# RWKV-7 scan of a diffusion trunk on one core: chunk batches of all head pairs in one series, merge inside a pair's first batch, transfers of the inverse on three queues

## The chip, the cores and the metric

One NeuronCore of one Trainium2 chip runs the whole program. The metric is the device time of one execution in microseconds (us); lower is better. Three runs of the kernel before gave 2060.2, 2059.9 and 2052.24 us, with a median of 2059.9 us.

## What is computed

Two trunk layers over 512 latent tokens (a 64-wide grid) and 256 context tokens of width 1024, all in float32. Layer 0 mixes by a bidirectional RWKV-7 recurrence (8 heads of 64) beside windowed attention, layer 1 by neighbourhood attention beside global attention. Each layer ends in a squared-ReLU MLP of width 4096, and each sub-layer is modulated by vectors that a product of the conditioning with `w_ada` gives. The part that matters here is the recurrence of layer 0, run once forwards and once backwards, the context tokens ahead of the latent ones:

```
def step(state, inp):
    r_t, w_t, k_t, v_t, kk_t, a_t = inp
    sa = jnp.einsum('bhvk,bhk->bhv', state, -kk_t)
    state = (state * w_t[:, :, None, :] + sa[..., None] * (kk_t * a_t)[:, :, None, :]
             + v_t[..., None] * k_t[:, :, None, :])
    return state, jnp.einsum('bhvk,bhk->bhv', state, r_t)
```

## The kernel before, in words

**The scan.** The 768 tokens are cut into 12 chunks of 64, and the 8 heads into 4 pairs (`p` = 0 to 3). Inside a chunk the recurrence is solved by matrix products, for which the inverse of a 64x64 triangular matrix is needed per chunk, head and direction. Three pieces of work make up a pair:

- `prep(p)` (L843) is a generator. Up to its mark FRONT it loads `r` and `k` and makes the norm, the decays and the rates. Up to READY it writes the factors `ar` and `bk` (L903, L908, L942, L945) and multiplies them on TensorE (L917), with the masked result in `XI` (L918). SP stores the 32x32 diagonal blocks of `XI` to DRAM in another layout (L925, four transfers) and loads them as `N` on 96 partitions (L928). From READY to MERGE VectorE inverts the blocks in 31 dependent steps of two instructions (L954, L955), copies the result transposed (L958), and SP stores both (L959, L960) and loads them back into `XI` and `xw` (L966, L967). After MERGE, TensorE and ScalarE join the 32x32 inverses to 64x64 ones (L974, an ACT copy, L982, an ACT copy).
- `chunks(p)` (L989) works in 4 batches of 3 chunks. Of a batch, `factors` (L1017), `masked` (L1046), `own` (L1062) and `solved` (L1071) come one batch ahead of `local` (L1082), `passed` (L1104) and the three `step`s (L1120), which hand the state on. `solved` is the first that reads the merged `XI`.
- `mix_out(p)` (L1177) takes the pair's output `y` and stores it. Pair 3 has `bonus` and `mix_last` in its place.

**Buffers.** `ar`, `bk`, `XI`, `wc`, `kds` lie in two sets, one for even and one for odd pairs. All of these products go through two PSUM tiles of two banks each (`wide()`, named `b` in the trace). `py` (two banks) gathers a pair's output, `pd` (one bank) carries the state product, and `ad` (one bank) belongs to the modulation.

**Order.** The kernel's text fixes each instruction's rank. The framework plans each engine's queue from these ranks, and every queue then runs in order, waiting where data or a buffer is late. Before the scan, the loop at L1484 runs `prep(1)` to READY and then the merge of pair 0 (L1486). For each pair, `for _ in cg` (L1532) walks the 37 yields of `chunks(p)`. At each it advances the background `bg` by RATE3 = 1.8 steps and the modulation `ag` by RATE4 = 0.7. The background takes turns between the inverse of pair p+1, `mix_out(p-1)` and `prep(p+2)` to FRONT. When the pair's chunks are through, `rest()` (L1542) runs `prep(p+2)` to READY and then the merge of pair p+1. Only then do the chunks of pair p+1 begin.

**The modulation.** `ada` (L332) streams 96 tiles of 512 KB of `w_ada` through three buffers on SP's queue (L341) and multiplies them (L353, L362); some 76 of them fall into the scan or just ahead of it.

Of the kernel before, what the change touches and what calls it, by code (L numbers as in the profile page):

```python
# [11 lines left out]
F32 = mybir.dt.float32  # L12
# [8 lines left out]
KT = 8  # L21
# [153 lines left out]
def trunk(ctx: ExitStack, tc: tile.TileContext, xT, cT, vec_d, wada, we, wo_in, wout, wf1, wf2, lw2_d, la2_d, lg2_d,  # L175
# [5 lines left out]
    def act(o, i, f=AF.Copy, **k):  # L181
        return S.activation(o, i, f, **k)  # L182
# [660 lines left out]
    def prep(p, R, rt, iv, sts, res):  # L843
# [77 lines left out]
        for d in range(2):  # L921
            for b in range(2):
                o = d * 64 + b * 32
                i0 = d * 48 + b * 24
                nc.sync.dma_start(nscr[p, i0:i0 + 24].rearrange("i s t -> s i t"), xv[o:o + 32, :, 32 * b:32 * b + 32])  # L925

        N = iv.tile([128, 32, 32], F32, name="N")
        nc.sync.dma_start(N[0:96], nscr[p])  # L928
        X = iv.tile([128, 32, 32], F32, name="X")
        G.memset(X[0:96], 0.0)  # L930
        G.memset(X[0:96].rearrange("p a b -> p (a b)")[:, 0::33], 1.0)
# [14 lines left out]
            yield QUIET  # L946
        G.tensor_tensor(kds, kds, kd, op=ALU.add)
        stt(kds, kds, VV["rk"][:, p:p + 1], r, op0=ALU.mult, op1=ALU.mult)
        yield READY
        for s in range(31):  # L950
            a, b = s + 1, 31 - s
# [4 lines left out]
            if s % 2:  # L956
                yield QUIET if s > QS else None
        V.tensor_copy(N[0:96].rearrange("p s i -> p i s"), X[0:96])  # L958
        nc.sync.dma_start(xscr[p], X[0:96])  # L959
        nc.sync.dma_start(tscr[p], N[0:96])  # L960
        w1 = rt.tile([128, T], F32, name="xw")
        for d in range(2):
            for b in range(2):
# [1 line left out]
                i0 = d * 48 + b * 24  # L965
                nc.sync.dma_start(xv[o:o + 32, :, 32 * b:32 * b + 32], xscr[p, i0:i0 + 24].rearrange("i s t -> s i t"))  # L966
            nc.sync.dma_start(w1[d * 64:d * 64 + 32].rearrange("s (i t) -> s i t", t=32), tscr[p, d * 48:d * 48 + 24].rearrange("i s t -> s i t"))  # L967
        res[p] = (AR, BK, XI, wc, kds)
        yield MERGE
        for q in range(2):  # L970
            pw = one()
# [14 lines left out]

    NB = 3

    def chunks(p, y, ct, pch, res):  # L989

# [7 lines left out]
        ch = (FWD, BWD)  # L998
        v = ct.tile([128, T], F32, name="v")
        nc.sync.dma_start(v, scr[3 + 3 * p + 2])  # L1000
        py = pch.tile([128, 2, 512], F32, name="py")
        pd = pch.tile([128, 128], F32, name="pd")
        yp = py[:, :, 0:384].rearrange("p h (c f) -> p h c f", f=64)
        B = [{} for _ in range(NCH // NB)]
        last = None
        env = {}
# [75 lines left out]
        def local(b):  # L1082

            BT, Z = B[b]["BT"], B[b]["Z"]
            pn = wide()[:, 0:NB * 128].rearrange("p (i d v) -> p i d v", i=NB, d=2)
            for i in range(NB):
                for d in range(2):
                    for h in range(2):
                        PE.matmul(pn[half(h), i, d], BT[:, h, d * NB + i, 0:64], Z[:, i, d, h], start=True, stop=True)
            N = B[b]["N"] = ct.tile([128, NB, 2, 64], F32, name="Nb", bufs=2)  # L1090
            act(N, pn)
            for i in range(NB):
# [27 lines left out]
        def step(b, i):  # L1120
            nonlocal X
            s = NB * b + i
            N = B[b]["N"][:, i]
            if not s:
                X = N
                return
            MQ, St = B[b]["MQ"], X
            if s < NCH - 1:
                for d in range(2):
# [11 lines left out]
        for b in range(nb + 1):  # L1141
            if b < nb:
                factors(b)
                yield
            if b:
                local(b - 1)
                yield
            if b < nb:
                masked(b)
                yield  # L1150
            if b:
                passed(b - 1)
                yield
            if b < nb:
                own(b)
                yield
            if b:
                step(b - 1, 0)
                yield
            if b < nb:  # L1160
                solved(b)
                yield
            if b:
                for i in range(1, NB):
                    step(b - 1, i)
                    yield
        act(y.rearrange("p c (h f) -> p h c f", h=2), yp)
        yield

    def centred(y):  # L1170

# [298 lines left out]
    with ExitStack() as p2:  # L1470
# [10 lines left out]
            if t != QUIET:  # L1481
                next(ag, None)
        gate = mix_gate(tl)
        for t in until(preps[1], READY):  # L1484
            next(ag, None)
        for t in preps[0]:  # L1486
            next(ag, None)
        for p in range(4):
            cg, n = chunks(p, y, ct, pch, res), 0

            def turns(*gs):
                gs = list(gs)
                while gs:
                    for g in list(gs):
                        t = next(g, gs)
                        if t is gs:
                            gs.remove(g)
                        else:
                            yield t

            def behind():
                def out():
                    return mix_out(p - 1, y, gate, tl, res) if p else iter(())
                if p < 3:
                    yield from turns(until(preps[p + 1], MERGE), out(), front(p + 2))
                else:
                    yield from out()
                    for x in mixs[::-1]:
                        x.close()
                    p3w["W"] = ffstream(p3w["x"].enter_context(pool("wp3")), 0)  # L1510
                    m0 = p3w["m0"] = p3w["m"].enter_context(pool("m0"))
                    p3w["last"] = m0.tile([128, T], F32, name="last")
                    yield from bonus(3, tl, res, gate, p3w["last"])
                    mh = m0.tile([128, KT, 256], F32R, name="mh")
                    ml = m0.tile([128, KT, 256], F32R, name="ml")
                    p3w["mh"] = mh, ml
                    for j in range(8):
                        for _ in range(3):
                            yield
                        p3w["W"].ahead(j + 1)  # L1520
                        if j in (5, 6):
                            a, b = ((4, 8), (0, 3))[j - 5]
                            if a:
                                mr = m0.tile([128, 4, 256], F32, name="mr")
                            else:
                                mr = tl.tile([128, T], F32, name="t", bufs=2).rearrange("p (k t) -> p k t", k=3)
                            nc.sync.dma_start(mr, mixd[a:b, :, 0:256].rearrange("k p t -> p k t"))
                            split(mh[:, a:b], ml[:, a:b], mr)
            bg = behind()
            due = [0.0, 0.0]  # L1530
            t = None
            for _ in cg:  # L1532
                n += 1
                due[0] += RATE3
                due[1] += RATE4
                while due[0] >= 1:
                    due[0] -= 1
                    next(bg, None)
                while due[1] >= 1:
                    due[1] -= 1  # L1540
                    next(ag, None)
            def rest():  # L1542
                if p < 2:
                    yield from until(preps[p + 2], READY)
                if p < 3:
                    yield from preps[p + 1]
            for t in itertools.chain(bg, rest()):
                due[1] += RATE5
                while due[1] >= 1:
                    due[1] -= 1  # L1550
                    next(ag, None)
        for _ in ag:
            pass
        end = mix_last(3, y, tl, p3w["last"], p3w["gate"], mk)
# [336 lines left out]
```

## Time and profile before

| what | value |
|---|---|
| runs | 2060.2, 2059.9, 2052.24 us; median 2059.9 us |
| profiled execution, its own time | 2055.19 us |
| its span, first to last instruction | 2053.4 us |
| TensorE busy (PE) | 1932.7 us, 94% of the span |
| VectorE busy (DVE) | 1124.7 us, 55% |
| ScalarE busy (ACT) | 817.0 us, 40% |
| GpSimd busy (POOL) | 122.2 us, 6% |
| mean granted clock of TensorE | 0.971 |
| DMA | 217.47 MB, 106 GB/s on the mean |

Everything below is from the profiled execution, with time counted from the start of its span. Busy time is the union of an engine's instructions. Matmuls overlap in the engine, so a busy PE can still wait between instructions. A sequencer's own work (waits, DMA issues) is not counted as busy. The granted clock is 1.00 at 2.4 GHz, and a stretch at 0.75 had half its time at 1.2 GHz.

### The profile page before, as it was taken

How to read it: one execution, taken by the hardware profiler on the slowest of the kernel's cores; microseconds unless marked ns; L12 is line 12 of the kernel's file. 1: busy time of each engine (PE TensorE's matmuls, PEld its weight loads, DVE VectorE, ACT ScalarE, POOL GpSimd, SP SyncE). 2: the span in 40 equal slices, each digit the busy share in tenths (PEclk: the TensorE clock that was granted, in tenths of full speed). 3: DMA queues.
4: the chain of work that ended last, by engine and by line, in shares of the span. 5: the costliest groups of instructions: out<-in, count | busy, mean ns of one | idle time of the engine just before them, and what ended most of it. 6: DMA issues, size and time to landing. Idle time of an engine off the chain costs nothing.

```text
span 2053.4 us, 38620 instructions
## 1 busy us (share of the span) xinstructions
PE 1932.7 (94%) x16412; PEld 1633.5 (80%) x16412; DVE 1124.7 (55%) x1999; ACT 817.0 (40%) x1531; POOL 122.2 (6%) x149
## 2 busy tenths in 40 slices
PE   6999988988888899999999999899999899999997
PEld 3878767666666897888888889898888798888887
DVE  6576477547464377233433345856575575444445
ACT  3466442534335244311322122435686645222332
POOL 1000011011100000000000000001021000000000
PEclk9999989999999999999999999999999999999998
DMA  7422334666634233211221021342111334322221
GB/s 309 149 65 78 108 109 129 209 195 207 207 126 145 71 112 132 73 61 42 83 72 62 32 83 42 103 151 68 51 39 37 123 102 166 102 83 82 97 88 42
DMA packets 112013, 217.47 MB, mean 106 GB/s; under 512 B 38496, under 2 KB 63968, under 8 KB 111328
## 3 DMA queue, kind: packets, MB, share of 16 engines
q1 hardware_dynamic: 96544, 191.66, 28.6%
q10 hardware_dynamic: 15296, 23.33, 3.2%
q8 instruction: 129, 2.11, 0.4%
q14 instruction: 44, 0.36, 0.1%
HBM read 184.29 MB, written 28.05 MB: 103 GB/s over the span
## 4 chain that ended last, share of the span: by engine, by line
PE 63%; DVE 7%; ACT 3%; issue 3%; DMA 2%; POOL 1%; POOLq 0%; ACTq 0%; DVEq 0%; SPq 0%
PE x L1588 45%; PE x L430 5%; PE ax L530 2%; PE ax L511 2%; PE b L1015 1%; PE b L493 1%; PE ad L353 1%; PE b L1077 1%; PE b L494 1%; DMA w_raw<-in_wada_dram 1%; DVE X L955 1%; DVE nacc L288 1%; ACT Z L182 1%; DVE pr L954 1%; POOL r L264 0%
## 5 line engine op out<-in xcount | busy, mean ns | idle before, releaser
L182 ACT ACTIVATE w_hi<-w_raw 128x1024 fp32r<-128x1024 f32 x183 | 192.3, 1058 | 484.1 <-PE x L1588 369.1
L225 DVE TENSOR_TENSOR w_lo<-w_raw,w_hi 128x1024 fp32r<-128x1024 f32 x181 | 220.8, 1223 | 194.6 <-ACT w_hi L182 193.0
L1588 PE MATMUL x<-fl,w_hi 128*128 128x256 f32 (+1 forms) x864 | 290.9, 338 | 3.9 <-DVE fl L1675 3.9
L1588 PE MATMUL x<-uh,w_hi 128*128 128x512 f32 (+1 forms) x864 | 286.7, 337 | 3.0 <-ACT uh L182 3.0
L1588 PE MATMUL x<-fh,w_lo 128*128 128x256 f32 (+1 forms) x864 | 289.4, 336 | 0.0
L1588 PE MATMUL x<-ul,w_hi 128*128 128x512 f32 (+1 forms) x864 | 287.9, 336 | 0.0
L1588 PE MATMUL x<-uh,w_lo 128*128 128x512 f32 (+1 forms) x864 | 287.6, 336 | 0.0
L1588 PE MATMUL x<-fh,w_hi 128*128 128x256 f32 (+1 forms) x864 | 286.9, 337 | 0.0
L1602 DVE TENSOR_TENSOR oa<-x,oa 128x512 f32<-128x512 f32 (+1 forms) x184 | 103.1, 563 | 207.9 <-PE x L1588 207.0
L430 PE MATMUL x<-uh,w_hi 128*128 128x256 f32 (+1 forms) x560 | 190.2, 340 | 1.6 <-ACT po L182 1.3
L430 PE MATMUL x<-uh,w_lo 128*128 128x256 f32 (+1 forms) x560 | 189.1, 338 | 0.0
L430 PE MATMUL x<-ul,w_hi 128*128 128x256 f32 (+1 forms) x560 | 188.5, 337 | 0.0
L1588 PEld LDWEIGHTS x<-fl,w_hi 128*128 128x128 f32 x864 | 164.3, 190 | 22.0 <-DVE fl L1675 4.3
L1588 PEld LDWEIGHTS x<-uh,w_hi 128*128 128x128 f32 x864 | 161.8, 189 | 21.1 <-ACT uh L182 3.9
L1588 PEld LDWEIGHTS x<-fh,w_lo 128*128 128x128 f32 x864 | 164.1, 190 | 17.9
L1588 PEld LDWEIGHTS x<-fh,w_hi 128*128 128x128 f32 x864 | 162.1, 190 | 20.0 <-ACT fh L182 2.5
L1588 PEld LDWEIGHTS x<-ul,w_hi 128*128 128x128 f32 x864 | 162.8, 189 | 17.7
L1588 PEld LDWEIGHTS x<-uh,w_lo 128*128 128x128 f32 x864 | 162.8, 189 | 17.6
L430 PEld LDWEIGHTS x<-uh,w_hi 128*128 128x128 f32 x560 | 107.5, 192 | 12.5 <-issue 2.7
L430 PEld LDWEIGHTS x<-uh,w_lo 128*128 128x128 f32 x560 | 107.7, 192 | 9.4 <-issue 1.2
L430 PEld LDWEIGHTS x<-ul,w_hi 128*128 128x128 f32 x560 | 107.8, 192 | 9.2 <-issue 1.3
L1674 DVE TENSOR_TENSOR rl<-rl 128x512 f32<-128x512 f32 (+1 forms) x108 | 59.3, 550 | 77.7 <-ACT fh L182 77.5
(304 smaller groups left out, 3398.7 us busy)
## 6 DMA issues: line engine op xcount, KB each, us to landing
w_raw<-in_wf_dram SPq DMA_DIRECT2D x128, 512.0 KB
w_raw<-in_wada_dram SPq DMA_DIRECT2D x96, 512.0 KB
w_raw<-in_we_dram SPq DMA_DIRECT2D x21, 512.0 KB
w_raw<-in_wo_in_dram SPq DMA_DIRECT2D x18, 512.0 KB
w_raw<-in_wout_dram SPq DMA_DIRECT2D x16, 512.0 KB
hsc<-h ACTq DMA_DIRECT2D x8, 1024.0 KB
scr<-po ACTq DMA_DIRECT2D x21, 384.0 KB
h<-hsc SPq DMA_DIRECT2D x7, 1024.0 KB
```

The lines of the kernel that those rows point to most:

```text
L182: return S.activation(o, i, f, **k)
L225: eng.tensor_tensor(o_lo, x, o_hi.bitcast(F32), op=ALU.subtract)
L288: V.tensor_reduce(acc, sq.rearrange("p k t -> p t k"), axis=AX.X, op=ALU.add)
L353: PE.matmul(ps[o:o + 32, 0:256], si[:, 2 * kp + k, :], w[:, k, j * 256:(j + 1) * 256], start=kp == 0, stop=kp == 3)
L430: PE.matmul(ps[:, 0:b - a], x, y, start=j == 0, stop=j == len(pairs) - 1)
L493: PE.matmul(ps[:, off:off + n], qs, kh, start=True, stop=False)
L494: PE.matmul(ps[:, off:off + n], qs, kl, start=False, stop=True)
L511: PE.transpose(pt[:, (kb - k0) * 128:(kb - k0 + 1) * 128], P[:, kb * 128:(kb + 1) * 128], ident)
L530: PE.matmul(po[h * 64:h * 64 + 64, 0:128], v(h, k), pts[h][:, k], start=k == 0, stop=k == n - 1)
L1588: PE.matmul(o, a, b, start=n == 0, stop=n == len(pairs) - 1)
L1602: tt(oa[:, m, tok], ps, oa[:, m, tok], op=ALU.add)
L1674: tt(r, r, r, op=ALU.mult)
```

## The change

The chunk stages become functions that `stages(p)` returns, and one generator `batches` walks 16 batches `g` of all pairs. In a round it takes `factors`, `masked`, `own`, `solved` of batch g and `local`, `passed` and the steps of batch g-1, whichever pair they belong to. When the first batch of a pair comes to `solved`, `batches` yields MERGE. Then the background is emptied, `prep(p+1)` to READY and the merge of pair p are emitted in turns, and a new background begins. In that background the inverse has two places in the turn. The loop that took `prep(1)` to READY ahead of the scan is gone; that part heads pair 0's background. `py` is allocated at the pair's first `local`, `pd` at each step. The four stores of `XI` move from SP's queue to ACT's, and the load of `N` and the two stores of the result move to POOL's.

```
-                nc.sync.dma_start(nscr[p, i0:i0 + 24].rearrange("i s t -> s i t"), xv[o:o + 32, :, 32 * b:32 * b + 32])
+                nc.scalar.dma_start(nscr[p, i0:i0 + 24].rearrange("i s t -> s i t"), xv[o:o + 32, :, 32 * b:32 * b + 32])
...
-        nc.sync.dma_start(N[0:96], nscr[p])
+        G.dma_start(N[0:96], nscr[p])
...
+        res[p] = (AR, BK, XI, wc, kds)
         yield READY
...
-        nc.sync.dma_start(xscr[p], X[0:96])
-        nc.sync.dma_start(tscr[p], N[0:96])
+        G.dma_start(xscr[p], X[0:96])
+        G.dma_start(tscr[p], N[0:96])
...
-    def chunks(p, y, ct, pch, res):
+    def stages(p, y, ct, pch, res, done_y):
...
-        py = pch.tile([128, 2, 512], F32, name="py")
-        pd = pch.tile([128, 128], F32, name="pd")
...
+            if s == NCH - 1:
+                act(y.rearrange("p c (h f) -> p h c f", h=2), yp)
+                done_y.append(p)
+        return factors, masked, own, solved, local, passed, step
+
+    def batches(y, ct, pch, res, done_y):
+        nb = NCH // NB
...
+        pairs[0] = stages(0, y, ct, pch, res, done_y)
+        for g in range(4 * nb + 1):
+            new, old = g < 4 * nb, 0 < g
+            work = [new and (FACTORS, g), old and (LOCAL, g - 1), new and (MASKED, g), old and (PASSED, g - 1), new and (OWN, g),
+                      old and (STEP, g - 1, 0), new and (SOLVED, g), old and (STEP, g - 1, 1), old and (STEP, g - 1, 2)]
+            for w in filter(None, work):
+                if w[0] == SOLVED and not g % nb:
+                    yield MERGE
+                f, b = of(w[1], w[0])
+                f(b, *w[2:])
                 yield
+                if w[0] == FACTORS and g % nb == nb - 1 and g < 4 * nb - 1:
+                    p = g // nb + 1
+                    pairs[p] = stages(p, y, ct, pch, res, done_y)
...
-        for t in until(preps[1], READY):
-            next(ag, None)
         for t in preps[0]:
             next(ag, None)
...
+        def behind(p):
+            if p < 3:
+                if p == 0:
+                    yield from until(preps[1], READY)
+                inverse = until(preps[p + 1], MERGE)
+                yield from turns(inverse, outputs(p - 1), inverse, front(p + 2))
+                return
...
+        for t in batches(y, ct, pch, res, done_y):
+            if t == MERGE:
+                for _ in bg:
+                    modulation(RATE5)
+                if p:
+                    for _ in turns(until(preps[p + 1], READY) if p < 3 else iter(()), preps[p]):
+                        modulation(RATE5)
+                bg, p = behind(p), p + 1
+                continue
+            modulation(RATE4)
+            due[0] += RATE3
+            while due[0] >= 1:
+                due[0] -= 1
+                next(bg, None)
```

`outputs(p)` is `mix_out(p)` once `done_y` holds p. RATE5 is 0.5.

## Rows read from the trace of the kernel before

**Rows 1.** The page's picture of the span in 40 equal slices of 51.3 us: busy tenths of TensorE, and the granted clock in tenths.

```profile
PE   6999988988888899999999999899999899999997
...
PEclk9999989999999999999999999999999999999998
```

**Rows 2.** Busy time by stretch, core 0. Columns: stretch and its length, busy us and instructions of PE, PEld, DVE, ACT and POOL, granted clock, DMA share, GB/s. The cuts are at 345.5 (end of the input products), 357.0 (first merge), 375.7, 469.0, 570.2 and 645.0 (factors of the second batch of pairs 0 to 3), and 434.1, 533.1 and 617.1 (end of the last `solved` of pairs 0 to 2). The last row is one batch of pair 3, from `factors` to `solved`, with no other work beside it.

```profile
345.50:357.00 11.50, 6.51 (x129) 4.32 (x127) 11.02 (x15) 2.09 (x6) 4.69 (x3) 0.70 0.63 192
357.00:375.70 18.70, 16.20 (x360) 13.49 (x356) 4.97 (x11) 9.43 (x19) 0.46 (x2) 0.73 0.60 166
375.70:434.10 58.40, 52.12 (x937) 36.53 (x940) 40.30 (x96) 25.14 (x44) 6.21 (x7) 1.00 0.71 226
434.10:469.00 34.90, 32.20 (x692) 21.52 (x685) 14.77 (x29) 11.81 (x26) 4.06 (x4) 0.90 0.66 195
469.00:533.10 64.10, 55.72 (x917) 41.15 (x918) 44.30 (x100) 26.89 (x47) 8.95 (x9) 0.92 0.59 191
533.10:570.20 37.10, 32.27 (x692) 21.29 (x684) 14.56 (x27) 11.93 (x26) 4.01 (x4) 0.91 0.67 207
570.20:617.10 46.90, 41.63 (x839) 31.75 (x840) 33.79 (x89) 15.25 (x33) 3.34 (x5) 1.00 0.42 129
617.10:645.00 27.90, 23.73 (x493) 18.66 (x486) 11.15 (x16) 14.12 (x26) 3.12 (x3) 0.82 0.35 102
...
672.50:683.00 10.50, 10.11 (x260) 9.15 (x260) 3.31 (x6) 4.16 (x9) 0.00 (x0) 1.00 0.01 3
```

**Rows 3.** Timeline of TensorE where the scan begins. Columns: start, length (us), engine, line, operation, shapes, count, and in brackets the idle time before it and what ended it.

```profile
345.90 0.50 PE L362 MATMUL ad<-con,adar 128*128 128x4 f32 x4
348.81 0.69 PE L917 MATMUL b<-ar,bk 64*64 64x64 f32 x8 [2.40 <-DVE po L1429]
...
357.05 1.99 PE L974 MATMUL b<-xw,XI 32*32 32x32 f32 x96
...
364.70 1.54 PE L1023 MATMUL b<-con,bk 128*128 128x128 f32 x6
```

**Rows 4.** Groups of TensorE's instructions by line between 434.1 and 469.0 us. Columns: line, engine, operation, tiles, shapes, count, then busy us and mean ns of one, then idle us before them.

```profile
L353 PE MATMUL ad<-w_raw,si 128*32 128x256 f32 x104 | 9.2, 429 | 1.7 <-DMA w_raw<-in_wada_dram 1.3 <-DVE mod L364 0.3
L917 PE MATMUL b<-ar,bk 64*64 64x64 f32 x96 | 3.3, 227 | 0.3 <-DVE ar L903 0.3
L982 PE MATMUL b<-XI,xw 32*32 32x32 f32 x96 | 2.5, 205 | 0.0
...
L974 PE MATMUL b<-xw,XI 32*32 32x32 f32 x96 | 1.9, 192 | 0.0
L362 PE MATMUL ad<-con,adar 128*128 128x4 f32 x12 | 1.8, 258 | 0.2 <-ACT adar L182 0.2
...
L1190 PE MATMUL b<-kds,con 128*128 128x512 f32 (+1 forms) x4 | 1.6, 512 | 0.0
```

**Rows 5.** The same view between 617.1 and 645.0 us.

```profile
L1190 PE MATMUL b<-kds,con 128*128 128x512 f32 (+1 forms) x4 | 2.8, 844 | 0.0
L982 PE MATMUL b<-XI,xw 32*32 32x32 f32 x96 | 2.4, 214 | 0.4 <-ACT xw L182 0.3
L974 PE MATMUL b<-xw,XI 32*32 32x32 f32 x96 | 2.2, 192 | 0.0
...
L1210 PE MATMUL b<-gl,lg 128*128 128x512 f32 (+1 forms) x4 | 1.6, 512 | 0.2 <-ACT Z L182 0.2
...
L1205 PE MATMUL b<-con,y 128*128 128x128 f32 x6 | 0.9, 282 | 0.0
```

**Rows 6.** Timeline of SP's queue: what it issued, and for how long it was occupied, around the store of `XI` of pairs 1, 2 and 3. A load of `w_raw` (L341) that waits for its buffer is counted in its row.

```profile
357.63 3.18 SPq L925 DMA_DIRECT2D nscr<-XI  x4
...
449.21 11.06 SPq L341 DMA_DIRECT2D w_raw<-in_wada_dram  x5
460.33 3.86 SPq L925 DMA_DIRECT2D nscr<-XI  x4
...
553.38 4.71 SPq L925 DMA_DIRECT2D nscr<-XI  x4
```

**Rows 7.** Timelines of DVE, SP and PE: the inverse of pair 3 from its last masked product to its merge.

```profile
550.31 0.68 DVE L918 TENSOR_TENSOR XI<-b,con 128x512 f32<-128x512 f32 x1
...
577.81 0.18 DVE L954 TENSOR_TENSOR pr<-X,N 96x31 f32<-96x31 f32 x1
...
609.94 0.33 SPq L959 DMA_DIRECT2D xscr<-X  x1
...
609.95 1.09 DVE L958 COPY N<-X 96x1024 f32<-96x1024 f32 x1
...
617.76 0.53 SPq L967 DMA_DIRECT2D xw<-tscr  x1
...
622.34 0.24 PE L974 MATMUL b<-xw,XI 32*32 32x32 f32 x2
```

**Rows 8.** What SP's queue waited for between 345 and 692 us: us in total, times, longest.

```profile
SPq L341 <- PE ad L353: 129.5, 49, 14.6
```

**Rows 9.** Groups by line between 357 and 692 us: the inverse on DVE (three pairs), and on POOL the copies of `v` that `factors` transposes.

```profile
L955 DVE TENSOR_TENSOR X<-X,pr 96x31 f32<-96x31 f32 (+15 forms) x93 | 31.6, 340 | 2.5
L954 DVE TENSOR_TENSOR pr<-X,N 96x31 f32<-96x31 f32 (+15 forms) x93 | 31.3, 336 | 2.3
...
L1038 POOL COPY vr<-v 128x192 f32<-128x192 f32 (+2 forms) x19 | 7.5, 409 | 150.7 <-PE b L1040 121.4 <-ACT w_hi L182 15.3 <-ACT BT L182 13.5
```

More of the change, by code (lines that the diff above doesn't have):

```diff
@@ L967, in prep @@
             nc.sync.dma_start(w1[d * 64:d * 64 + 32].rearrange("s (i t) -> s i t", t=32), tscr[p, d * 48:d * 48 + 24].rearrange("i s t -> s i t"))
-        res[p] = (AR, BK, XI, wc, kds)
         yield MERGE
@@ L1000, in chunks @@
         nc.sync.dma_start(v, scr[3 + 3 * p + 2])
-        py = pch.tile([128, 2, 512], F32, name="py")
-        pd = pch.tile([128, 128], F32, name="pd")
-        yp = py[:, :, 0:384].rearrange("p h (c f) -> p h c f", f=64)
         B = [{} for _ in range(NCH // NB)]
@@ L1091, in local @@
             act(N, pn)
+            if not b:
+                py = pch.tile([128, 2, 512], F32, name="py")
+                env["yp"] = py[:, :, 0:384].rearrange("p h (c f) -> p h c f", f=64)
+            yp = env["yp"]
             for i in range(NB):
@@ L1126, in step @@
                 return
-            MQ, St = B[b]["MQ"], X
+            MQ, St, yp = B[b]["MQ"], X, env["yp"]
             if s < NCH - 1:
+                pd = pch.tile([128, 128], F32, name="pd")
                 for d in range(2):
@@ L1138, in step, with of @@
                         PE.matmul(yp[half(c % 2), h, c // 2], MQ[half(h), d, i, 64:128], St[half(h), d], start=False, stop=s == NCH - 1)
-        nb = NCH // NB
-        for b in range(nb + 1):
-            if b < nb:
-                factors(b)
-                yield
[L1145 to L1168, printed above, removed]
+            if s == NCH - 1:
[3 more added lines that the diff above has]
+    def batches(y, ct, pch, res, done_y):
+        nb = NCH // NB
+        pairs = {}
+        def of(g, stage):
+            return pairs[g // nb][stage], g % nb
+        FACTORS, MASKED, OWN, SOLVED, LOCAL, PASSED, STEP = range(7)
+        pairs[0] = stages(0, y, ct, pch, res, done_y)
[8 more added lines that the diff above has]
+                f(b, *w[2:])
+                yield
+                if w[0] == FACTORS and g % nb == nb - 1 and g < 4 * nb - 1:
+                    p = g // nb + 1
+                    assert p in res
+                    pairs[p] = stages(p, y, ct, pch, res, done_y)
     def centred(y):
@@ L1483, in trunk @@
         gate = mix_gate(tl)
-        for t in until(preps[1], READY):
-            next(ag, None)
         for t in preps[0]:
             next(ag, None)
[L1488 to L1551, printed above, removed]
@@ new lines, in turns, with outputs @@
+        def turns(*gs):
+            gs = list(gs)
+            while gs:
+                for g in list(gs):
+                    t = next(g, gs)
+                    if t is gs:
+                        gs.remove(g)
+                    else:
+                        yield t
+        done_y = []
+        def outputs(p):
+            if p >= 0:
+                while p not in done_y:
+                    yield
+                yield from mix_out(p, y, gate, tl, res)
+        def behind(p):
[5 more added lines that the diff above has]
+                return
+            yield from outputs(p - 1)
+            for x in mixs[::-1]:
+                x.close()
+            p3w["W"] = ffstream(p3w["x"].enter_context(pool("wp3")), 0)
+            m0 = p3w["m0"] = p3w["m"].enter_context(pool("m0"))
+            p3w["last"] = m0.tile([128, T], F32, name="last")
+            yield from bonus(3, tl, res, gate, p3w["last"])
+            mh = m0.tile([128, KT, 256], F32R, name="mh")
+            ml = m0.tile([128, KT, 256], F32R, name="ml")
+            p3w["mh"] = mh, ml
+            for j in range(8):
+                for _ in range(3):
+                    yield
+                p3w["W"].ahead(j + 1)
+                if j in (5, 6):
+                    a, b = ((4, 8), (0, 3))[j - 5]
+                    if a:
+                        mr = m0.tile([128, 4, 256], F32, name="mr")
+                    else:
+                        mr = tl.tile([128, T], F32, name="t", bufs=2).rearrange("p (k t) -> p k t", k=3)
+                    nc.sync.dma_start(mr, mixd[a:b, :, 0:256].rearrange("k p t -> p k t"))
+                    split(mh[:, a:b], ml[:, a:b], mr)
@@ new lines, in trunk, with modulation @@
+        due, bg, p = [0.0, 0.0], iter(()), 0
+        def modulation(rate):
+            due[1] += rate
+            while due[1] >= 1:
+                due[1] -= 1
+                next(ag, None)
+        for t in batches(y, ct, pch, res, done_y):
[12 more added lines that the diff above has]
+                next(bg, None)
@@ L1552, in trunk @@
+        for _ in bg:
+            modulation(RATE5)
         for _ in ag:
```

## The prediction

> **What bounds the kernel now.** I read the slices first [rows 1]. TensorE is at 9 tenths nearly everywhere, but at 8 in the six slices in a row from 411 to 719 us, the ninth to the fourteenth; the clock's tenths are too coarse to tell anything there. That region is the scan. The stretches [rows 2] then show what a batch costs without company: 10.5 us, of which PE is busy 10.11. No other engine is near full there (DVE 3.31, ACT 4.16), so a batch is a sequence of small products, each of which needs the copy of an earlier one. Last I read what PE does where one pair hands over to the next [rows 4, 5], because the change rearranges those places.
>
> Between the last `solved` of a pair and the second `factors` of the next (434.1 to 469.0, 533.1 to 570.2, 617.1 to 645.0), the work is exactly one batch: `local`, `passed` and the steps of the old one, and `factors`, `masked`, `own` and `solved` of the new. To it come the other products. In the first handover they are modulation 9.2 + 1.8, L917 3.3, merge 1.9 + 2.5, L1190 1.6, together 20.3 us [rows 4]. With the batch that is 30.8 us, and the stretch takes 34.9: **4.1 us over**. The second has the same 692 instructions and takes 37.1: **6.3 over**. The third has no modulation and no L917, but 2.8 + 2.4 + 2.2 + 1.6 + 0.9 = 9.9 us of its own [rows 5]; 20.4 against 27.9: **7.5 over**. Here the old pair runs dry, the merge waits for its copies, and the new pair fills up.
>
> **The change part by part.**
>
> *Start of the scan.* A product buffer is free at 348.81, when DVE has read the last input product; the merge of pair 0 starts at 357.05, behind the L917 of pair 1 [rows 3]. With that part gone from in front, the merge can start 8.2 us sooner. What it displaces moves into pair 0: 96 L917 at 3.3 us and three tiles of modulation, 24 instructions at 9.2/104 us each, 2.1 us; together 5.4. PE stands idle in pair 0 for 2.5 + 6.3 = 8.8 us [rows 2], so from all to none of it is hidden, and the gain lies between 8.2 and 2.8. I take the middle, 5.5, since that idle time is scattered in small waits. VectorE's part, 11.0 us of 11.5, falls where it is idle for 13.7 and then 18.1 us [rows 2]; the inverse of pair 1 comes behind it, with a whole pair to go.
>
> *One series.* At a handover the old batch's products now lie between the new one's, as in the clean batch. The 4.1 + 6.3 + 7.5 = 17.9 us can go. They need not: if the merge, now emitted in one go ahead of `solved`, waits as it did, nothing goes. I take all of it, since the clean batch alternates in the same way and has 0.4 us idle. What is late next is the inverse (first rival).
>
> *Clock.* The granted clock is 0.90, 0.91 and 0.82 in the three handovers and 1.00 in the clean batch [rows 2]. If it stayed up there, (1 - clock) x length comes back: 3.5 + 3.3 + 5.0 = 11.8 us. PE also waits there, so at least nothing and at most this; I take a third, 3.9.
>
> *Stores of `XI` on ACT.* On SP the four took 3.18, 3.86 and 4.71 us [rows 6], 11.75 in three pairs. For that long ACT copies nothing, and behind them stand the copies of `own` and `solved` that PE needs. ACT is busy 11.81 of 34.9 us [rows 2], so a part meets idle time. Between 0 and -11.75 I take half, -5.9. That they no longer stand behind the modulation on SP (11.06 us in pair 2's case [rows 6]; SP waits 129.5 us for products of the modulation [rows 8]) helps the inverse alone.
>
> *Three transfers on POOL.* No transfer of the trace goes out from there. POOL is busy 4.06 of 34.9 us; behind these transfers stand the 0.41 us copies of `v` [rows 9], which `factors` needs. If the planned order suits, the cost is 0. If POOL waits for each landing as long as the stores take to issue, it is another 11.75. Sooner service could save as much again. I take 0, by POOL's idle share; the high end is the third rival.
>
> For pair 3 the store of the inverse is issued at 609.94, and VectorE's copy of 1.09 us starts beside it at 609.95 [rows 7]. The Trainium skill ("SBUF — State Buffer", "SBUF: two separate sides") says that GpSimd, which writes the descriptors of such a transfer, is locked out while VectorE runs a two-port float32 copy. By that rule up to 1.1 us a pair would be lost, 3.3 in three, and the sum would be 3.3 less if the inverse set the pace; no transfer of this trace tests it.
>
> *Inverse at double pace.* It changes ranks alone: 1.8 x 1/2 = 0.9 steps a yield for 0.6, so 15 yields are spent by yield 17. Its 93 + 93 instructions take 62.9 us, 21.0 a pair [rows 9], and pair 3's took 32.1 from 577.81 [rows 7]; it can come down to 21 at the cost of copies that PE needs. On the path: 0. `mix_out` and `prep` fall to 0.45 steps each and still end inside the pair. `pd` at each step waits for the same addition as the next step; `py` waits for the copy of `y`, with the whole of `factors` between; `res` earlier costs nothing. The load of `v` has a batch, 10.5 us, of cover; behind a 14.6 us wait of SP [rows 8] 4 us would show.
>
> *Sum.* 5.5 + 17.9 + 3.9 - 5.9 = 21.4 us. Against the profiled execution's own 2055.2 that gives 2033.8. The median of the runs lies 4.7 us above it, which would give 2038.5. I forecast **2036**, between them.
>
> **The rivals.**
>
> *The inverse becomes the bound.* Pair 3's takes from 551.0 to 622.34, or 71.3 us: 26.8 until it starts, 32.1, and 12.4 to the merge [rows 7]. In the new order its first product comes behind the merge of pair 2 (4.4 + 3.3 us [rows 4]), so two merges are at least 79 us apart if no piece shrinks. Pair 2's products need 46.9 us [rows 2], a handover batch of 10.5 and those 7.7, so 65. Then 14 us of the gain are lost: 2033.8 + 14 = **2048**. Against it: 26.8 us is long for a transfer out and in, and both queues and ranks aim at it; with 13 less there and 5 less in the inverse the 79 become 61, below 65.
>
> The Trainium skill ("DMA: Bandwidth & Descriptors", "Issuing engines are not separate DMA queues") says that issuing from several engines saves only the sequencer's time. By that rule the transfers themselves would be no sooner, and this rival would hold; the trace shows SP occupied for 11.06 us ahead of one of these stores, which is sequencer time.
>
> *Nothing to be had at the handovers.* PE is busy 32.20 of 34.9 us there. If these records are work and the planner had already drawn the neighbours in, only the start gains, and ACT's stores take it: 2055.2 - 5.5 + 5.9 = **2056**.
>
> *Slower: POOL's queue.* The load of `N` stands in POOL's order behind stores that have yet to land, and the stores of the inverse behind VectorE's 31 steps. If a copy of `v` is planned behind either, `factors` waits and PE with it. At a batch, 10.5 us, for each of three pairs, and with ACT's whole 11.75, that is 43.3 us against gains of 23.4: 2055.2 + 19.9 = **2075**. It decides from a loss of 7.8 us a pair on. For it: the order is planned, and no transfer has been seen on POOL. Against it: VectorE's order is planned by the same ranks, so both shift together.
>
> **How the numbers follow.** The forecast's case has 0.60, the inverse 0.15, nothing 0.12, POOL 0.13. A measurement of this kernel can tell about 0.5%, or 10.3 us, from no change. Of the forecast's case 0.55 lies beyond that. The inverse's 2048 lies at the edge: 0.06 faster, 0.09 same. So faster 0.61, same 0.05 + 0.09 + 0.12 = 0.26, slower 0.13. All gains whole and no loss give 8.2 + 17.9 + 11.8 = 37.9, 2017 by the profiled time. Upwards the range takes in the inverse and the empty case with the runs' 4.7 us: 2061 and a little. It reaches from 2016 to 2063; outside it are most of the POOL case and the chance of more than all.
>
> **What would show it.** Right: the first L974 starts near 349; from the last `solved` of a pair to the second `factors` of the next there are 28 to 31 us, 24 in the last case; the clock there is above 0.95; L974 of pair 3 finds its data landed. Wrong: an idle PE ahead of L974, released by the load of `xw` (the inverse); L1040 or L1077 released by POOL or ACT for several us (the queues); handovers as long as now. The end of the scan should come some 21 us sooner, with everything behind it shifted as a block.

## The result, and the profile after

The changed kernel is slower: median 2075.46 us (4 runs, 2073.92 to 2077.97) against 2056.62 us (4 runs), ratio 1.0094, 95% interval 1.0067 to 1.0121, or some 19 us. The forecast of 2036 us was wrong; the time is that of the third rival (2075), but by luck, since its mechanism is not what the runs show. In the profiled execution (span 2073.5 us) the scan's last state product ends at 712.1 us, before at 690.7; behind it everything is shifted as a block.

The page's slices of TensorE and its granted clock, as [rows 1]:

```profile
PE   6999978887988899999999999899999899999997
...
PEclk9999989888998999999999999999999999999998
```

Stretches of core 0 with the columns of [rows 2], cut at the same events: first merge 354.8, `factors` of the second batches 373.3, 471.9, 574.3, 656.3, last `solved` 437.0, 545.6, 632.0, end of the scan 712.1.

```profile
354.80:373.30 18.50, 13.58 (x349) 10.44 (x349) 11.62 (x14) 8.69 (x17) 4.83 (x5) 0.72 0.67 226
373.30:437.00 63.70, 53.82 (x936) 41.42 (x934) 35.61 (x78) 25.40 (x45) 6.06 (x6) 0.87 0.32 104
437.00:471.90 34.90, 30.25 (x672) 21.66 (x672) 17.01 (x41) 11.43 (x25) 3.03 (x6) 0.80 0.63 180
471.90:545.60 73.70, 60.01 (x929) 41.68 (x930) 46.38 (x104) 26.68 (x47) 15.21 (x13) 0.91 0.61 183
545.60:574.30 28.70, 26.64 (x672) 19.30 (x664) 9.74 (x22) 10.04 (x24) 0.47 (x2) 1.00 0.59 189
574.30:632.00 57.70, 49.75 (x896) 35.70 (x898) 39.89 (x97) 16.83 (x36) 8.91 (x9) 0.91 0.64 206
632.00:656.30 24.30, 23.26 (x529) 18.57 (x530) 4.22 (x11) 10.83 (x24) 0.47 (x2) 0.86 0.54 168
656.30:712.10 55.80, 42.13 (x887) 35.22 (x885) 29.47 (x38) 25.83 (x43) 3.71 (x3) 0.91 0.33 108
```

The handovers (third, fifth and seventh row) take 34.9, 28.7 and 24.3 us for 34.9, 37.1 and 27.9 [rows 2]: 12 us are gained. The stretches ahead of each take 63.7, 73.7 and 57.7 for 58.4, 64.1 and 46.9: 25.7 lost. The last row takes 55.8, and the same stretch of the kernel before (645.0 to 690.7) 45.7: another 10.1 lost. From 250 us to the scan's end PE is idle for 462.1 - 391.7 = 70.4 us, before for 51.5, and the granted clock is 0.89 for 0.92.

What VectorE, TensorE and SP waited for between 250 and 713 us (us in total, times, longest):

```profile
DVE pr L955 <- DMA N<-nscr: 31.7, 4, 12.7
...
PE ad L353 <- DMA w_raw<-in_wada_dram: 11.5, 8, 6.5
PE b L1208 <- DVE y L1204: 8.4, 1, 8.4
PE b L1193 <- DVE AK L1050: 6.5, 1, 6.5
...
PE b L1012 <- DVE AK L1050: 4.5, 1, 4.5
...
PE b L974 <- DMA xw<-tscr: 2.6, 2, 2.3
...
SPq L967 <- DMA xscr<-X: 23.6, 4, 17.4
```

Three of these are new. VectorE stands for `N`, which it never did before. PE stands for a `w_ada` load ahead of the modulation for 6.5 us in one piece while the input products run. And in the last row of the stretches PE stands 8.4 us at L1208 for pair 2's output `y`, which `mix_out` scales on VectorE (L1204); e3, e11 and e14 below have that wait too (8.3 to 8.5 us), e1 and e8 do not. SP's wait for the stores of the inverse was 9.5 us before. The timeline shows the first two: the load waited for is one of four issued from 275.12 on, and in pair 1 the first inverse step stands ahead of the mask that PE needs.

```profile
274.43 1.50 PE L353 MATMUL ad<-w_raw,si 128*32 128x256 f32 x24
282.48 1.08 PE L353 MATMUL ad<-w_raw,si 128*32 128x256 f32 x8 [6.55 <-DMA w_raw<-in_wada_dram]
...
275.12 8.82 SPq L341 DMA_DIRECT2D w_raw<-in_wada_dram  x4
...
385.49 2.66 ACTq L925 DMA_DIRECT2D nscr<-XI  x3
...
395.16 0.56 POOL L928 DMA_DIRECT2D N<-nscr  x1 [18.32 <-PE b L1049]
...
399.16 0.19 DVE L955 TENSOR_TENSOR pr<-X,N 96x31 f32<-96x31 f32 x1 [12.70 <-DMA N<-nscr]
...
399.74 0.55 DVE L1050 TENSOR_TENSOR AK<-b,con 128x384 f32<-128x384 f32 x1
...
400.35 1.01 PE L1012 MATMUL b<-con 128*128 128x192 f32 x2 [4.48 <-DVE AK L1050]
```

The stores of pair 1 leave ACT until 388.15; POOL issues the load of `N` at 395.16, and VectorE goes on at 399.16. Between the mask of `XI` (L918) and the first step VectorE runs 10, 3, 4 and 7 other instructions in pairs 0 to 3; before it ran 14, 11, 13 and 15 (counted in the two traces). So the step stands earlier in VectorE's queue, and the data came no sooner.

### The profile page after: what moved, and what is told of

Same layout as the page of the kernel before. It is cut to its first block, busy times and chain, and to the rows that moved or that the text cites. A ratio compares the mean times of both kernels' runs of the same rounds, so it can differ in the third digit from the quotient of the medians.

```text
span 2073.5 us, 38626 instructions
## 1 busy us (share of the span) xinstructions
PE 1935.7 (93%) x16412; PEld 1638.8 (79%) x16412; DVE 1123.6 (54%) x1999; ACT 815.1 (39%) x1531; POOL 130.8 (6%) x161
## 4 chain that ended last, share of the span: by engine, by line
PE 61%; DVE 5%; ACT 3%; issue 2%; DMA 1%; POOL 1%; ACTq 0%; POOLq 0%; DVEq 0%; SPq 0%
PE x L1598 45%; PE x L430 5%; PE ax L530 2%; PE ax L511 2%; PE b L493 1%; PE b L494 1%; PE b L1012 1%; PE ad L353 1%; PE b L1074 1%; DVE nacc L288 1%; DVE w_lo L225 0%; POOL rs L264 0%; ACT P L182 0%; DVE h L310 0%; POOL r L264 0%
## 5 line engine op out<-in xcount | busy, mean ns | idle before, releaser
L1598 PEld LDWEIGHTS x<-uh,w_hi 128*128 128x128 f32 x864 | 162.4, 190 | 21.2 <-ACT uh L182 3.9
L1598 PEld LDWEIGHTS x<-fh,w_hi 128*128 128x128 f32 x864 | 162.5, 190 | 19.9 <-ACT fh L182 2.5
```

The costliest lines, as they stand in the source:

```text
L1598: PE.matmul(o, a, b, start=n == 0, stop=n == len(pairs) - 1)
```

## The experiments

Eighteen runs; "before" and "after" say which kernel was edited. Differences in us are (ratio - 1) x 2055. "N" is VectorE's wait for `N`, "w" PE's wait for `w_ada` from 250 us to the end of the scan, "w0" its part ahead of 350 us, all in us from the waits of each run's profile. e10 and e13 invert other numbers and e18 and e19 modulate by others; their instructions are those of the kernel before.

| run | stores of `XI` | ratio to before, 95% | us | N | w | w0 |
|---|---|---|---|---|---|---|
| before | SP | 1 | 0 | 0 | 5.7 | 0 |
| e12_ready_late | SP | 0.9961 (0.9941 to 0.9981) | -8.0 | 1.2 | 5.6 | 0 |
| e16_behind_sp | SP | 0.9977 (0.9961 to 0.9994) | -4.7 | 1.4 | 1.7 | 0 |
| e7_inverse_out | SP | 1.0000 (0.9979 to 1.0021) | 0 | 0 | 5.3 | 0 |
| e8_series | SP | 1.0011 (0.9991 to 1.0031) | 2.3 | 0.2 | 9.9 | 0 |
| e11_stores_sp | SP | 1.0032 (1.0010 to 1.0054) | 6.6 | 4.1 | 4.7 | 0 |
| e1_sp | SP | 1.0034 (1.0014 to 1.0053) | 7.0 | 0 | 7.8 | 0 |
| e6_load | SP | 1.0038 (1.0018 to 1.0059) | 7.8 | 6.7 | 7.1 | 0 |
| after | ACT | 1.0094 (1.0067 to 1.0121) | 19.3 | 31.7 | 11.5 | 6.5 |
| e14_after_pinned | ACT | 1.0103 (1.0068 to 1.0137) | 21.2 | 6.7 | 12.9 | 6.7 |
| e3_pace | ACT | 1.0106 (1.0085 to 1.0127) | 21.8 | 29.8 | 11.3 | 6.8 |
| e15_behind_act | ACT | 1.0051 (1.0033 to 1.0068) | 10.5 | 2.7 | 15.5 | 4.8 |
| e9_pinned | ACT | 1.0122 (1.0084 to 1.0159) | 25.1 | 3.2 | 21.0 | 4.2 |
| e5_stores | ACT | 1.0126 (1.0079 to 1.0174) | 25.9 | 25.5 | 14.1 | 4.0 |
| e2_queues | ACT | 1.0136 (1.0119 to 1.0153) | 27.9 | 26.4 | 16.7 | 5.7 |
| e4_ready | ACT | 1.0152 (1.0135 to 1.0169) | 31.2 | 26.9 | 14.0 | 5.2 |
| e13_free_sp | SP | 1.0047 (1.0026 to 1.0068) | 9.7 | 0 | 6.3 | 0 |
| e10_free | ACT | 1.0032 (1.0010 to 1.0053) | 6.6 | 0.6 | 16.1 | 4.7 |
| e19_light_sp | SP | 0.9917 (0.9896 to 0.9939) | -17.1 | 0 | 0.7 | 0 |
| e18_light_act | ACT | 0.9972 (0.9959 to 0.9984) | -5.8 | 19.9 | 9.4 | 3.0 |

**Which part of the change.** e1 (after, all transfers on SP), e2 (before, all four moved), e3 (after, single pace), e4 (after, READY of pair 1 ahead again).

```
e1 -G.dma_start(N[0:96], nscr[p])
   +nc.sync.dma_start(N[0:96], nscr[p])
   ...
e2 -nc.sync.dma_start(N[0:96], nscr[p])
   +G.dma_start(N[0:96], nscr[p])
   ...
e3 -yield from turns(inverse, outputs(p - 1), inverse, front(p + 2))
   +yield from turns(inverse, outputs(p - 1), front(p + 2))
e4 +for t in until(preps[1], READY):
   +    next(ag, None)
    for t in preps[0]:
   ...
   -if p == 0:
   -    yield from until(preps[1], READY)
```

> The changed kernel with all four kinds of transfer of the inverse back on SP; the series of batches, READY of pair 1 behind the merge of pair 0 and the double pace stay. Theory Q (queues): the load of N from POOL lands 4 to 8 us after its issue and some 7 us after the stores, later than the planned place of the first inverse step; VectorE stands at it (27.2 us in three places of the changed kernel) and the masks of PE's products stand behind, and SP stands 17 us for a store that POOL issues late. Then most of the 21 us between the two kernels goes: I expect 2050 to 2060 us and no wait of VectorE for N over 2 us. Rival S (series): the late READY of pair 1 and the one series set the end of the inverse, whoever issues: 2068 to 2078 us, merge of pair 1 still at about 453 us. Rival D (double pace): as S, with VectorE's order at fault: 2068 us or more, waits of PE for masks as now.

> The kernel before with the four kinds of transfer moved to ACT and POOL as in the change, nothing else. Theory Q: it alone costs 10 to 20 us: 2067 to 2077 us, with VectorE waiting for N in it. Rivals S and D: the queues cost nothing by themselves: 2052 to 2062 us.

> The changed kernel with the inverse at single pace (one step a turn). Theory Q: the place of the first step does not move much, so the wait for N stays and the time is within 5 us of the changed kernel: 2070 to 2080 us. Rival D: the steps no longer crowd VectorE: 2060 us or less. Rival S (the inverse bounds the pair): it gets later: 2080 us or more.

> The changed kernel with READY of pair 1 ahead of the merge of pair 0 again, as in the kernel before. Rival S: the merge of pair 1 comes at about 448 in place of 453 us and the 4.5 us wait in pair 0 goes; 8 us for READY in front come back: 2068 to 2076 us at best 2065. Theory Q: the wait for N goes in pair 1 alone (its load has a batch more of cover) and stays in pairs 2 and 3: 2068 to 2078 us. If it falls below 2062, the move of READY was the cause.

Most of it is the queues: alone they cost 27.9 us, and without them the change costs 7.0 for 19.3. The double pace does nothing that shows (e3 beside after). With READY ahead again (e4) it gets 12 us worse, so that move was a help.

**Which transfer, and the series alone.** e5, e6 and e7 move one kind of transfer in the kernel before; e8 is the change with SP's transfers, single pace and READY ahead (the edits of e1, e3 and e4 together).

```
e5 -nc.sync.dma_start(nscr[p, i0:i0 + 24] ...
   +nc.scalar.dma_start(nscr[p, i0:i0 + 24] ...
e6 -nc.sync.dma_start(N[0:96], nscr[p])
   +G.dma_start(N[0:96], nscr[p])
e7 -nc.sync.dma_start(xscr[p], X[0:96])
   -nc.sync.dma_start(tscr[p], N[0:96])
   +G.dma_start(xscr[p], X[0:96])
   +G.dma_start(tscr[p], N[0:96])
```

> The kernel before with the stores of XI on ACT alone. With all four kinds of transfer moved the kernel before got 27 us slower; this tells how much of it is the stores'. Theory N (the load of N from POOL is the cause, by VectorE's wait for it): within 5 us of the kernel before. Rival A (the stores hold ACT and what stands behind them): 6 to 12 us slower.

> The kernel before with the load of N on POOL alone. Theory N: 12 to 25 us slower, with VectorE waiting for N some 20 us in sum. Rival X (the stores of the inverse from POOL are the cause, by SP's wait for them): within 5 us of the kernel before. Rival T (no single transfer does it, only their sum): 5 to 10 us slower, as the other two.

> The kernel before with the stores of the inverse (X and its transpose) on POOL alone. Theory N: up to 6 us slower, by SP's wait for them (31 us in sum with all moved) and the w_ada loads behind it. Rival X: 12 us slower or more, with PE waiting for w_raw over 12 us. Rival T: 5 to 10 us.

> The changed kernel without its other three parts: transfers on SP, READY of pair 1 ahead of the merge of pair 0, single pace; what is left is the series of batches. Prediction: 18 us of the handovers go and some clock comes back: 2030 to 2042 us. Rival H (nothing to be had at the handovers): within 5 us of the kernel before, 2048 to 2058 us. Rival M (the emptied background and the merge ahead of solved cost more than the series brings): 2060 us or more.

Theory N (the load of `N` from POOL) fell: the stores on ACT cost 25.9 us, the load on POOL 7.8, the stores of the inverse nothing. In e5 PE's idle time from 250 us to the scan's end grows from 51.5 to 71.4 us and its busy time, for the same products, from 389.2 to 398.7, at a granted clock of 0.88 for 0.92; so a third of the 29.4 us by which the scan ends later is busy time. And the series alone is worth nothing (2.3 us slower, interval -1.8 to 6.4). Its stretches, handovers first (435.0, 534.9 and 616.1 on), then the rest from the first merge to the scan's end, with the columns of [rows 2]:

```profile
435.00:466.70 31.70, 29.78 (x688) 20.49 (x685) 9.91 (x23) 10.94 (x27) 0.47 (x2) 0.93 0.62 200
534.90:563.10 28.20, 26.96 (x682) 19.08 (x678) 10.02 (x21) 10.99 (x27) 0.47 (x2) 1.00 0.64 211
616.10:639.10 23.00, 19.03 (x482) 16.22 (x476) 7.77 (x13) 11.82 (x24) 2.74 (x3) 0.85 0.49 136
355.90:435.00 79.10, 69.56 (x1293) 51.00 (x1290) 44.91 (x107) 33.90 (x63) 6.83 (x9) 0.92 0.68 205
466.70:534.90 68.20, 57.37 (x934) 41.27 (x934) 48.78 (x107) 27.05 (x47) 12.68 (x10) 0.92 0.64 192
563.10:616.10 53.00, 43.10 (x839) 32.48 (x836) 39.32 (x95) 15.74 (x33) 7.75 (x6) 0.97 0.42 124
639.10:690.00 50.90, 41.71 (x886) 34.16 (x884) 26.02 (x34) 24.30 (x41) 0.69 (x2) 1.00 0.33 111
```

The handovers are 82.9 us for 99.9 [rows 2], 17.0 less. The other stretches are 251.2 for 234.1 (with 46.0 for the last, 645.0 to 691.0, in the kernel before): 17.1 more. PE's busy time falls by 12.4 at the handovers and rises by 7.3 between them (the products of `mix_out`, such as L1193, moved there); its idle time falls by 4.6 and rises by 9.8, with the waits for `w_ada` up from 5.7 to 9.9. The handovers got shorter, and the time was given back inside the pairs.

**How the stores cost it.** e9: e5 with the first step of pairs 1 to 3 held behind VectorE's mask `BT`. e10: e5 with `N` from `w_ada`. e11: after with only the stores on SP. e12: before with READY of pair 1 behind the merge of pair 0.

```
e9  +for _ in range(2 if p else 0):
    +    yield
    -tt(tv, X[0:96, 0:a, s:s + 1] ...
    +with tc.issue_after(LB[-1].ins) if p and not s else nullcontext():
    +    tt(tv, X[0:96, 0:a, s:s + 1] ...
e10 -nc.sync.dma_start(N[0:96], nscr[p])
    +nc.sync.dma_start(N[0:96], wada[0, p, 0][0:96].rearrange(...))
e11 -nc.scalar.dma_start(nscr[p, i0:i0 + 24] ...
    +nc.sync.dma_start(nscr[p, i0:i0 + 24] ...
e12 -for t in until(preps[1], READY):
    -    next(ag, None)
    ...
    +if p == 0:
    +    yield from until(preps[1], READY)
     if p < 3:
         yield from turns(until(preps[p + 1], MERGE), out(), front(p + 2))
```

> The kernel before with the stores of XI on ACT (which alone cost 26 us) and with the first step of the inverse of pairs 1 to 3 held behind VectorE's second mask (BT) of the running batch, about where the kernel before had it; for this the step is also emitted two turns later. ACT's queue holds the stores as before. Theory P (the planned place: with the stores on ACT the first step is put ahead of the masks and VectorE stands there for N): most of it goes, at most 10 us slower than the kernel before, wait for N under 8 us in sum. Rival A (ACT is held by the stores, and what stands behind them is late): 18 to 30 us slower as without the hold.

> The kernel before with the stores of XI on ACT, and N loaded from w_ada in place of the stored blocks, so that nobody waits for the stores (the inverse is then of other numbers; the same 124 + 124 instructions). Theory P: no wait of VectorE for N, within 10 us of the kernel before or faster. Rival A: ACT is held as long as before: 18 us slower or more.

> The changed kernel with only the stores of XI back on SP; the load of N and the stores of the inverse stay on POOL. Theory P: of the changed kernel's loss 12 us were the queues', mostly the stores'; the load on POOL keeps up to 8: 2058 to 2068 us, wait for N under 10 us. Rival X (POOL's transfers cost in the series what they did not in the old order): 2068 us or more.

> The kernel before with READY of pair 1 behind the merge of pair 0, as the change has it, and nothing else. Prediction's step: the merge of pair 0 comes 8 us sooner and the displaced work is partly hidden: 2047 to 2052 us with the kernel before at 2055. Rival B (the inverse of pair 1 then ends too late for the merge of pair 1, as in the changed kernel, where PE waited for it): 2055 to 2065 us.

In e9 the wait for `N` is gone but for 3.2 us in pair 0 and no time came back, so P (the planned place of the first step) fell. Its timeline at the first merge shows what else stands behind the stores (lines of that kernel are shifted: L354 is the modulation, L980 and L988 the merge):

```profile
363.76 1.71 PE L980 MATMUL b<-xw,XI 32*32 32x32 f32 x96
369.64 1.07 PE L354 MATMUL ad<-w_raw,si 128*32 128x256 f32 x8 [4.17 <-DMA w_raw<-in_wada_dram]
373.30 1.02 PE L363 MATMUL ad<-con,adar 128*128 128x4 f32 x4 [2.58 <-ACT adar L183]
...
362.85 0.33 ACTq L928 DMA_DIRECT2D nscr<-XI  x1
...
364.70 8.07 ACTq L928 DMA_DIRECT2D nscr<-XI  x3
...
372.45 0.31 ACTq L928 DMA_DIRECT2D nscr<-XI  x1
372.87 0.38 ACT L183 ACTIVATE adar<-ad 128x256 f32<-128x256 f32 x1 [7.33 <-DMA nscr<-XI]
373.27 1.98 ACT L183 ACTIVATE xw<-b 32x384 f32<-32x384 f32 x4
```

Three stores occupy ACT's queue for 8.07 us, and the merge's copies `xw` come behind them. Little of that is issuing: the last of the three is the row at 372.45 (from a view that begins at 367), the other two take 1.98 us, and for 5.8 us the queue waits for the pair's first store, issued at 362.85, whose completion semaphore the last one uses again and which lands at 372.43. From the first L974 to the last L982 it takes 16.4, 19.9 and 20.4 us in pairs 0 to 2, against 7.7, 7.0 and 8.6 before. But e10 has nearly the merges of e5 (15.6, 11.2 and 14.1 us for 16.5, 11.2 and 15.9) and is only 6.6 us slower. In the changed kernel four stores leave ACT in 2.1 to 3.6 us, without such a wait; e11 tells that they cost 12.7 us there (19.3 - 6.6, some 7 either way) and POOL's transfers nothing on balance (6.6 beside e1's 7.0, some 6 either way). e12 beats both kernels, 2047.79 against 2052.97 us in its comparison; of the runs below that compute the same numbers only e16 does so too, by less.

**Controls.** e13: e10 with the stores on SP. e14: after with the first step held as in e9, six turns later. e15: before with the stores on ACT and READY of the next pair behind the merge in every pair; e16: the same on SP. e18: e5 with an eighth of each `w_ada` load; e19: the same on SP.

```
e14 +for _ in range(6 if p else 0):
    +    yield
    ...
e15 -if p < 2:
    -    yield from until(preps[p + 2], READY)
     if p < 3:
         yield from preps[p + 1]
    +if p < 2:
    +    yield from until(preps[p + 2], READY)
    ...
e18 -w = wa.tile([128, 2, 512], F32, name="w_raw")
    -eng.dma_start(w, todo.pop(0))
    +w = ws[len(todo) % n]
    +eng.dma_start(w[:, :, 0:64], todo.pop(0)[:, :, 0:64])
```

> Control to the run with N from w_ada and the stores on ACT (6.6 us slower than the kernel before): the same with the stores on SP, where nothing waits for them either. Theory H (ACT is held at the stores, and the copies of the running merge, xw and XI, stand behind them): 15 us or more faster than with the stores on ACT, that is 2040 to 2048 us. Theory P (only the wait for N costs): the same as on ACT, 2056 to 2064 us.

> The changed kernel with all its queues, and the first step of the inverse of pairs 1 to 3 held behind the running batch's masks (for this it is emitted six turns later). In the series the stores of the next pair come behind the merge's copies, so Theory H has little to hold there: it expects that the stores' 13 us of the changed kernel come from elsewhere. Theory P: VectorE's wait for N falls from 27 us to below 8 and 6 to 13 us come back: 2058 to 2066 us. If the wait goes and the time stays at 2070 to 2078 us, P is false here too.

> The kernel before with the stores of XI on ACT, and READY of the next pair (so its stores too) behind the merge in all pairs. Theory H: the merge's copies no longer stand behind the stores; of the 26 us that the stores cost at most 10 are left against the same order on SP. Theory P or a plain loss by ACT's time: 18 us or more are left.

> Control: the same order (READY of the next pair behind the merge) with the stores on SP. With READY late for pair 1 alone the kernel before got 8 us faster. For pairs 2 and 3 the merge comes 4 to 8 us sooner and the inverse later by as much; pair 3's inverse had 4 us to spare: 2040 to 2054 us.

> The kernel before with the stores of XI on ACT, and every w_ada load of the scan cut to an eighth of its bytes (64 of 512 columns, into three fixed tiles that are zeroed first); the products stay, so the modulation is of other numbers. To be held against the same with the stores on SP. Theory S (with the stores on another queue the planned order lets w_ada loads, stores and N run beside each other; they share the DMA engines and land later than planned, and PE stands at the modulation's products and VectorE at N): with light loads the difference ACT to SP falls from 26 us to below 10. Rival A (ACT is held for as long, whatever SP loads): the difference stays at 18 us or more.

> Control: the kernel before with the light w_ada loads and the stores of XI on SP. PE waited 5.7 us for w_ada in the scan of the kernel before, and SP's loads of w_ada stood 129.5 us for products: 2040 to 2056 us.

Where nobody waits for the stores, ACT costs no more than SP (e10 and e13): H (copies standing behind the stores on ACT) fell as a plain hold. With the merge out of the way ACT still costs 15.2 us over SP (e15 and e16), so H explains at most the other 10.7 of the 25.9. In the changed order the held first step took 25 us of waits for `N` away and gave nothing (e14): P is false there too. What all ten runs with the stores on ACT share is the wait for `w_ada`: 9.4 to 21.0 us for 0.7 to 9.9 with SP, of it 3.0 to 6.8 in one piece while the input products run, where no run with SP has any. But the length of this wait is not the price: e10 waits 16.1 us and e13 6.3, and e10 is no slower. With light loads the stores cost 11.3 us (0.9972 - 0.9917) in place of 25.9. Theory S (transfers side by side share the DMA engines and land late) expected under 10. By the intervals the two figures are 6 to 16 and 16 to 36 us, so roughly half of the cost goes with the light loads. They change PE's order too: ahead of the modulation's 257th product stand 2446 other products in e19 for 2538 in the kernel before. Bytes and order are not told apart.

## Why the prediction was wrong

Two steps failed. The sum promised a gain of 21.4 us, and the kernel lost 19.3. Of the 40.7 us between, about 34 lie in the series, the start and the clock (27.3 promised, 7.0 lost in e1), and about 7 in the stores (-5.9 promised, -12.7 in e11).

**"Stores of `XI` on ACT" failed on size and on mechanism.** It took -5.9 within 0 to -11.75, from the time that SP was occupied [rows 6]. Measured: -12.7 in the changed kernel (e11), at the bound, and -25.9 alone (e5), well beyond it. The price is not the issue time, since e10 pays the same and is no slower than e13. While SP issued them, the stores stood in one order with the `w_ada` loads. With the stores on ACT the modulation's products stand sooner in PE's queue (2312 other products ahead of the 257th in e5, 2538 before), the inverse's first step sooner in VectorE's, and both engines then wait for data that comes no sooner. That these waits are the price is not shown: without the wait for `N` the time stayed (e9, e14), and a longer one for `w_ada` cost nothing (e10). Shown is that the move of the stores costs, and that light `w_ada` loads take roughly half of it away (e18, e19); by what path is open. The Trainium skill ("DMA: Bandwidth & Descriptors", "Issuing engines are not separate DMA queues") says that transfers from different issuing engines run on the same 16 DMA engines and interleave. e18 and e19 fit that, and no run measures it by itself. The prediction used that rule against the gain and not for a loss.

**"One series: I take all of it" failed too, and it was the largest term.** The handovers did become 17.0 us shorter in e8, as the 17.9 said, but the total moved by 2.3 us, and not downwards. Only 11.7 of those 99.9 us were idle [rows 2]; to call the excess over a clean batch lost was wrong, since the products that left the handover were needed elsewhere and the other stretches had idle time of their own to grow. Nor is the work of a handover exactly one clean batch: the trace has 40 and 32 products of L1138 and L1131 in the second of them for 24 and 24 in the clean batch, one state step more, some 1.1 us. "Nothing to be had at the handovers", at 0.12, was the right rival for this term.

**Start of the scan:** 5.5 within 8.2 to 2.8 was right: 8.0 alone (e12, interval 3.9 to 12.1). In the changed kernel the first merge is 2.3 us sooner (354.8 for 357.05 [rows 3]), in e1 and e11 10.2 and 7.7; the 6.55 us wait of PE while the input products run takes most of the difference.

**Clock:** 3.9 expected; in the changed kernel it fell, 0.89 for 0.92. The term also counts in part what the series already had: the excess was taken over a clean batch at 1.00, so it holds what the lower clock costs that batch. With the series alone (e8) it is 0.93, 1.00 and 0.85 in the handovers for 0.90, 0.91 and 0.82 [rows 2], and no higher in the longest of the other stretches (0.92 for 0.93 in the first): too little to see in the time.

**POOL:** 0 was right for the series. The third rival reached 2075 with 31.5 us lost to POOL, 11.75 to ACT and 23.4 gained; measured are about 0, 12.7 and a loss of 7.0, so only its price for ACT came true, and its sum by luck. By its own sum it also turns into a loss from 3.9 us a pair on, (23.4 - 11.75) / 3, not from 7.8. Its argument against itself, that VectorE's order shifts along, was false, as the 3 to 7 instructions ahead of the first step show. In the old order the load of `N` costs 7.8 us with 6.7 us of new waits. The lock between GpSimd and VectorE, which the prediction cites from the Trainium skill ("SBUF — State Buffer", "SBUF: two separate sides") and estimates at up to 3.3 us, does not show: e7 is at 0 within 4.3 us either way, which is too wide to exclude it. **Double pace:** 0 was right.

**The inverse as the bound** held once: in pair 1 of the changed kernel PE waits 2.3 us at L974 for `xw`. In pairs 2 and 3 the last load of `xw` is issued at 539 and 632 us and the merge begins at 559.5 and 642.6.

Together: 7.0 for series, late READY and double pace on SP, 12.7 for the stores, about 0 for POOL: 19.3. Besides the path by which the stores cost, two things stay open: why late READY, which gains 8.0 us alone, and the series, whose loss of 2.3 is within its noise, lose 7.0 when they come together (with the double pace, whose part on SP was not run alone), and what the 11.3 us are that the stores cost beside light loads.

## What to carry to other kernels

Do not price a transfer moved to another queue by its issue time alone: look at what it ran in order with before, and at what now stands sooner in the other queues. A stretch that exceeds the clean case is a gain only as far as its idle time goes, and only if the rest of the stage does not give it back. When a change has several parts, run the small one alone: here moving READY gained 8 us, and the rest hid it.

## What was not expected of the hardware

Transfers issued by POOL occupied it 0.51 to 0.96 us and landed 3.6 to 7.6 us after their issue (12 transfers of the changed kernel). Three stores of 96 KB occupied ACT's queue for 8.07 us where four took SP 3.0 to 4.7 us; 5.8 of it was a wait for an earlier store of the same queue, which landed 9.6 us after its issue (e9). Cutting the `w_ada` loads to an eighth gained 17.1 us in a kernel in which PE waited only 5.7 us for them. And loading `N` from data that are long there, so that the inverse can begin early, cost 9.7 us (e13); no run here says why.
